# A delta-rule scan whose GpSimd arithmetic goes to VectorE, with joint loads and stored zeros, and one clearing tied behind the first gather of an expert stage

## The chip, the cores and the metric

The kernel runs on one core of a Trainium2 chip. The metric is the device time of one execution in microseconds (us), as the median of several. Engine names: PE is TensorE (matrix products; PEld its weight loads), DVE is VectorE, ACT is ScalarE, POOL is GpSimd, SP is SyncE, which here only issues DMAs. Each engine works through its own instructions in a fixed order; an instruction that waits holds up all behind it on its engine.

## The reference

One layer of a streaming encoder over 2048 tokens of width 1024, all in float32:

```
h = rms_norm(x) * (1 + scale1) + shift1
proj = h @ w_in                      # q,k,v of attention | q,k,v,z,beta,a of the delta rule | branch gates
o_a = diff_attention(q, k, v, lam)   # 4 heads, two 64-wide maps each, ALiBi bias, block-causal mask
o_b = gated_delta_rule(...)          # 4 heads, state 128 x 128 per head, chunks of 64 tokens
merged = gate_a * (o_a @ w_branch_a) + gate_b * (o_b @ w_branch_b)
x = x + gate1 * (merged @ w_out)
x = x + gate2 * hier_moe(rms_norm(x) * (1 + scale2) + shift2)   # top 2 of 32 SwiGLU experts
```

The delta rule of one chunk, per head:

```
lower = strict_lower(beta_i * (k @ k^T) * decay);  a_mat = I + lower
u, w  = solve(a_mat, [v * beta, k * beta * exp(gcum)])
v_new = u - w @ state
o     = (q * exp(gcum)) @ state + (lower_incl(q @ k^T) * decay) @ v_new
state = state * exp(gcum_last) + (k * exp(gcum_last - gcum))^T @ v_new
```

The expert layer sorts the tokens by expert, gathers their rows, runs `(silu(x @ w1[e]) * (x @ w3[e])) @ w2[e]` and adds the weighted results to the output rows.

## The kernel before

Large products run as three products of rounded parts (`hh`, `hl` of the activations, `ghi`, `glo` of the weights). The stages follow each other: projections (to about 780 us of the trace), `gates_and_gdn` (780 to 1300), attention with the merge of the branches (to 1900), output projection and router (to 2105), the routing tables, and from about 2150 the experts (`phase5`).

`gates_and_gdn` interleaves two kinds of work. A gate unit is a group of 24 PE matmuls `pg` of 512 columns (lines 554 to 556) with little work on other engines; they fill PE. The delta rule works on 16 blocks `t` of 128 tokens (two chunks each):

- `gdn_a(t)` (line 640) loads `kq` (keys and queries), makes the decay `e` on ACT, `el = e * sl` and `eu = e * triu` (masked copies) on POOL (lines 653, 654), then multiplies the products `pk` from PE into `el` and `eu` on DVE (lines 663, 665), and stores them to DRAM as `nL` and `qkm` from the SP queue.
- `lanes(hf)` (line 670), after the eighth and the sixteenth block, reads 32 x 32 diagonal blocks of `nL` of eight blocks `t` and inverts them by a recurrence on DVE: 31 pairs of a product `lQ` (line 682) and a sum (line 684), each needing the one before. The inverses `X` and their transposes `L` are stored to DRAM as `TB` and `UB`.
- `scan(t)` (line 694) loads these as `T` and `U` (tags sT, sU; eight DMAs of 16 KB, and eight clearings of 32 x 128 on POOL for the blocks beside the diagonal), `nw`, `kv` (keys, values), `zq`, and `kq` again; scales keys and values on POOL (lines 715, 716); completes the inverse by small PE products to 64 x 64, copied on POOL into `W` (lines 739, 740); then on the path from block to block: `pks` (keys times state), `R` on DVE (line 758), `pv` on PE (line 762), `vn` on ACT (line 764), `pS` on PE (line 767), the new state `S` on DVE (line 770). The output is normalised on DVE and ACT, transposed on PE and stored as `oTB` from the SP queue.

`nw`, `kv`, `zq` and the three tiles of `lanes` share five buffers (tag c4). `el`, `vn` and `oT` share the one buffer of tag el, `eu` and `o` that of tag eu (`GB = 1`). The order of instructions on each engine is set by a scheduler ahead of the run, not by the text.

In `phase5`, the row numbers of the first expert block (`sgi`) come out of the routing tables, a gather DMA from the POOL queue (line 1584) fetches its rows into `xfirst`, POOL clears a small tile `g` (line 1587), and a DVE copy of it, `gone` (line 1589), is set behind the routing's last instruction. The DVE work of the first expert (`ow`, and the first rounding remainders `low`, line 1620) is ordered behind `gone`. PE transposes `xfirst` (line 1694), ACT and DVE split it (`xh`, lines 1698 and 1699), and the expert's matmuls follow.

Of the kernel before, what the change touches and what calls it, by code (L numbers as in the profile page):

```python
# [9 lines left out]
F32 = mybir.dt.float32  # L10
# [4 lines left out]
ALU = mybir.AluOpType  # L15
# [66 lines left out]
class K:  # L82
# [65 lines left out]
    def phase1(self, late):  # L148
        tc, nc, I = self.tc, self.nc, self.i
        h3 = late.enter_context(tc.tile_pool(name="h3", bufs=1, reuse_waits="tile"))  # L150
        d = self.d = {}
        for n in ("q_hi", "q_lo", "k_hi", "k_lo"):
            d[n] = self.dram(n, (H, P, S))
        d["v_tok"] = self.dram("v_tok", (S, 512))
        d["gqT"] = self.dram("gqT", (H, P, S))
        d["gkT"] = self.dram("gkT", (H, P, S))
        d["gk_tok"] = self.dram("gk_tok", (S, 512))
        d["gv_tok"] = self.dram("gv_tok", (S, 512))
        d["zs"] = self.dram("zs", (S, 512))
        d["mods"] = self.dram("mods", (4, D))  # L160
        d["gate"] = self.dram("gate", (2, KT, P, S))
        with ExitStack() as ctx:
# [105 lines left out]
            for j in range(2):  # L268
# [8 lines left out]
                if j == 0:  # L277
                    first = make_h(0, xs.pop(0))
# [157 lines left out]
            def gdn_unit(which, w, h, s, ct):  # L436
# [37 lines left out]
                if which != "q":  # L474
                    nc.scalar.dma_start(
                        d[f"g{which}_tok"][s * TS:(s + 1) * TS, h * P:(h + 1) * P]
                        .rearrange("(a p) b -> p a b", p=P),
                        tok.rearrange("p (a b) -> p a b", b=P))
                if which != "v":
                    yield 1  # L480
                    yield 1
                    t2 = ps.tile([P, 512], F32, tag="tp", bufs=3, name=f"c2{which}{h}{s}")
                    for t in range(4):
                        nc.tensor.transpose(t2[:, t * P:(t + 1) * P], tok[:, t * P:(t + 1) * P], self.ident)
                    o = wk.tile([P, 512], F32, tag="e3", name=f"co{which}{h}{s}")
                    nc.scalar.copy(o, t2)
                    nc.scalar.dma_start(d[f"g{which}T"][h, :, s * TS:(s + 1) * TS], o)

# [73 lines left out]
    def gates_and_gdn(self, ctx, sm, ps, hxp, hh, hl):  # L562
# [5 lines left out]
        qk = self.dram("qkm", (NT, P, H, P))  # L568
        TB = self.dram("TB", (NT, H, 4, 32, 32))
        UB = self.dram("UB", (NT, H, 4, 32, 32))  # L570
        c = E(tc.tile_pool(name="cg", bufs=1, reuse_waits="tile"))
# [9 lines left out]
        def sm64(name):  # L581
            return c.tile([P, NT, H], F32, name=name)
# [9 lines left out]
        bt = lambda a: a.unsqueeze(1).to_broadcast([P, NT, H])  # L592
        beta, g, x, e1, e2, e3 = (sm64(n) for n in ("beta", "g", "gx", "ge1", "ge2", "ge3"))
        A.activation(beta, self.ba[:, :, 0:4], AF.Tanh, scale=0.5)
# [7 lines left out]
        V.tensor_scalar(out=e2, in0=e2, scalar1=-1.0, scalar2=None, op0=ALU.add)  # L602
        z0 = sm64("gz0")
        V.tensor_scalar(out=z0, in0=e2, scalar1=0.0, scalar2=None, op0=ALU.is_equal)
# [26 lines left out]
        G.memset(S0, 0.0)  # L631
        state = [S0]

        def load_kq(t):
            kq = hxp.tile([P, H, 2, P], F32, tag="hx", name=f"kq{t}")
            for j, n in enumerate(("gkT", "gqT")):
                nc.sync.dma_start(kq[:, :, j, :], d[n][:, :, t * P:(t + 1) * P].rearrange("h p t -> p h t"))
            return kq

        def gdn_a(t):  # L640
# [8 lines left out]
            A.activation(e, e, AF.Exp, scale=-1.0)  # L649
            el = gd.tile([P, H, P], F32, tag="el", name=f"el{t}", bufs=GB)  # L650
            eu = gd.tile([P, H, P], F32, tag="eu", name=f"eu{t}", bufs=GB)
            mb = lambda a: a.unsqueeze(1).to_broadcast([P, H, P])
            G.tensor_tensor(out=el, in0=e, in1=mb(self.sl), op=ALU.mult)
            G.tensor_tensor(out=eu, in0=e, in1=mb(self.triu), op=ALU.mult)
            yield 1
            for hp in range(2):
                pk = psg(f"pk{t}_{hp}").rearrange("p (h j t) -> p h j t", h=2, j=2)
                for hh in range(2):
                    h = 2 * hp + hh
                    PE.matmul(pk[:, hh], kq[:, h, 0, :], kq[:, h], start=True, stop=True)  # L660
                for hh in range(2):
                    h = 2 * hp + hh
                    V.scalar_tensor_tensor(out=el[:, h, :], in0=pk[:, hh, 0, :], scalar=nbeta[:, t, h:h + 1],
                                           in1=el[:, h, :], op0=ALU.mult, op1=ALU.mult)
                V.tensor_tensor(out=eu[:, 2 * hp:2 * hp + 2, :], in0=pk[:, :, 1, :],
                                in1=eu[:, 2 * hp:2 * hp + 2, :], op=ALU.mult)
            nc.sync.dma_start(nL[t].rearrange("h i j -> i h j"), el)
            nc.sync.dma_start(qk[t], eu)

        def lanes(hf):  # L670
            X = gd.tile([P, 32, 32], F32, tag="c4", name=f"lX{hf}", bufs=5)
            L = gd.tile([P, 32, 32], F32, tag="c4", name=f"lL{hf}", bufs=5)
            Q = gd.tile([P, 1024], F32, tag="c4", name=f"lQ{hf}", bufs=5)
            src = nL[8 * hf:8 * hf + 8].rearrange("t h r c -> (t h) r c")
# [14 lines left out]
            for dst, src in ((TB, X), (UB, L)):  # L689
                dv = dst[8 * hf:8 * hf + 8].rearrange("t h b r c -> (t h) b r c")  # L690
                for b in range(4):
                    nc.sync.dma_start(dv[:, b], src[32 * b:32 * b + 32])

        def scan(t):
            c4 = lambda n: gd.tile([P, 2, H, P], F32, tag="c4", name=f"{n}{t}", bufs=5)
            nw, kv, zq = c4("nw"), c4("kv"), c4("zq")
# [11 lines left out]
            nc.sync.dma_start(qm, qk[t])  # L708
# [52 lines left out]
            for h in range(H):  # L761
                PE.matmul(pv[:, h * P:(h + 1) * P], W[:, h, :], R[:, h, :], start=True, stop=True)
            vn = gd.tile([P, H, P], F32, tag="el", name=f"vn{t}", bufs=GB)
            A.copy(f2(vn), pv)
# [9 lines left out]
            for h in range(H):  # L774
                PE.matmul(pq[:, h * P:(h + 1) * P], kq[:, h, 1, :], S0[:, h, :], start=True, stop=True)
            o = gd.tile([P, H, P], F32, tag="eu", name=f"o{t}", bufs=GB)
            for h in range(H):
# [17 lines left out]
            for h in range(H):  # L795
                PE.transpose(tp[:, h * P:(h + 1) * P], o[:, h, :], self.ident)
            oT = gd.tile([P, H, P], F32, tag="el", name=f"oT{t}", bufs=GB)
# [767 lines left out]
    def phase5(self):  # L1565
# [3 lines left out]
        with ExitStack() as ctx:  # L1569
# [13 lines left out]
            first = wk.tile([P, D], F32, tag="x", name="xfirst")  # L1583
            G.indirect_dma_start(out=first[0:P // 2], out_offset=None, in_=d["h2"],
                                 in_offset=bass.IndirectOffsetOnAxis(ap=self.gi[0:P // 2, b0:b0 + 1], axis=0))

            G.memset(g0, 0.0)
            with tc.issue_after(self.routed.ins):
# [261 lines left out]
```

## Time and profile before

| what | value |
|---|---|
| median of 3 executions | 2963.07 us (2959.84 to 2963.28) |
| profiled execution, its own time | 2976.06 us |
| its span in the trace | 2974.1 us |
| mean granted TensorE clock | 0.976 of full speed |
| PE / DVE / ACT / POOL busy | 94% / 72% / 45% / 12% |
| mean DMA rate | 189 GB/s |

The profile is of one execution. The span runs from the first to the last instruction. [...] Idle time of an engine costs only where another one waits for its next instruction.

### The profile page before, as it was taken

The numbers are of one execution on the slowest core, as the hardware profiler recorded it, in microseconds if no ns is written. First come the engines' busy times: TensorE is split into PE (matmuls) and PEld (weight loads), VectorE is DVE, ScalarE is ACT, GpSimd is POOL, SyncE is SP. The second block draws the span as 40 slices with busy tenths as digits, with TensorE's granted clock in tenths as the row PEclk, the third lists the DMA queues.
The fourth block names the chain that finished last, engine by engine and source line by source line (L and its number), as shares of the span: only waits on it lengthen the run. The fifth ranks groups of instructions, "written<-read, shape, count | busy, mean of one in ns | idle before, by whom it ended". The sixth has DMA issues, their size and how long they took to land. (4 is left out here: it accounts for less than half of the span.)

```text
span 2974.1 us, 43868 instructions
## 1 busy us (share of the span) xinstructions
PE 2793.6 (94%) x14845; PEld 2268.2 (76%) x14845; DVE 2130.4 (72%) x5098; ACT 1326.5 (45%) x2409; POOL 356.7 (12%) x354
## 2 busy tenths in 40 slices
PE   5999999999999899999999999999689999999997
PEld 4888778788787777777787887788567777777776
DVE  7567668996355643457888786687787797897896
ACT  4522213332322243356765564322255465664664
POOL 2300000000122122200000000100032121122211
PEclk8999999999999999999999999999789999999999
DMA  6333572211455465487776756744488898998995
GB/s 227 111 99 114 164 228 72 93 61 54 117 164 147 139 184 164 137 175 173 182 180 168 186 145 174 223 158 153 150 296 273 265 338 274 328 333 266 310 356 165
DMA packets 426243, 561.18 MB, mean 189 GB/s; under 512 B 56520, under 2 KB 240920, under 8 KB 426016
## 3 DMA queue, kind: packets, MB, share of 16 engines
q1 hardware_dynamic: 340560, 440.87, 48.3%
q10 hardware_dynamic: 73744, 75.53, 7.4%
q0 software_dynamic: 11712, 41.95, 6.1%
q8 instruction: 119, 1.95, 0.3%
q14 instruction: 108, 0.88, 0.1%
HBM read 436.06 MB, written 122.18 MB: 188 GB/s over the span
## 5 line engine op out<-in xcount | busy, mean ns | idle before, releaser
L1620 DVE TENSOR_TENSOR low<-raww,hiw 128x1024 fp32r<-128x1024 f32 x384 | 445.8, 1218 | 20.1 <-ACT hiw L1618 19.1
L1618 ACT CAST hiw<-raww 128x1024 fp32r<-128x1024 f32 x384 | 379.2, 1049 | 133.7 <-PE py L1673 68.3
L554 PE MATMUL pg<-hh,ghi 128*128 128x512 f32 x512 | 209.7, 410 | 2.5 <-ACT ghi L545 2.5
L338 PE MATMUL mma<-whi,hh 128*128 128x512 f32 x512 | 209.5, 409 | 2.7 <-ACT hh L245 1.4
L1010 DVE CUSTOM_DVE_ANT_0 sp<-sc,M 128x512 f32<-128x512 f32 (+1 forms) x320 | 183.7, 606 | 38.2 <-PE sc L1008 37.5
L556 PE MATMUL pg<-hh,glo 128*128 128x512 f32 x512 | 207.3, 405 | 0.0
L555 PE MATMUL pg<-hl,ghi 128*128 128x512 f32 x512 | 207.1, 404 | 0.0
L340 PE MATMUL mma<-whi,hl 128*128 128x512 f32 x512 | 203.6, 398 | 1.1 <-DVE hl L255 0.8
L339 PE MATMUL mma<-wlo,hh 128*128 128x512 f32 x512 | 202.4, 395 | 0.4 <-DVE wlo L261 0.4
L1015 ACT ACTIVATE sp<-sp,mx 128x128 f32<-128x128 f32 (+15 forms) x128 | 153.9, 1203 | 51.8 <-DVE mx L1013 45.9
L1034 PEld LDWEIGHTS av<-V,aT 128*128 128x128 f32 x1088 | 138.2, 192 | 33.8 <-ACT aT L1032 26.3
L348 PE MATMUL mmb<-hh,whi 128*128 128x512 f32 x384 | 156.4, 407 | 5.3 <-ACT whi L260 5.3
L1034 PE MATMUL av<-V,aT 128*128 128x128 f32 x1088 | 152.3, 282 | 9.2 <-ACT aT L1032 8.1
L350 PE MATMUL mmb<-hh,wlo 128*128 128x512 f32 x384 | 151.7, 395 | 0.5 <-POOL wlo L261 0.4
L349 PE MATMUL mmb<-hl,whi 128*128 128x512 f32 x384 | 151.0, 393 | 0.0
L1007 PE MATMUL sc<-K,qd 128*128 128x512 f32 (+1 forms) x320 | 130.7, 412 | 6.9 <-DVE mx L1010 2.9
L1032 ACT COPY aT<-tr 128x512 f32<-128x512 f32 (+3 forms) x160 | 78.4, 517 | 99.0 <-PE tr L1030 98.6
L1008 PE MATMUL sc<-K,ql 128*128 128x512 f32 (+1 forms) x320 | 117.7, 375 | 1.7 <-DMA ql<-q_lo 1.7
L1672 PE MATMUL py<-hiw,dh 128*128 128x512 f32 x272 | 108.8, 400 | 10.5 <-ACT dh L1663 10.3
L338 PEld LDWEIGHTS mma<-whi,hh 128*128 128x128 f32 x512 | 97.7, 191 | 25.1 <-ACT hh L245 1.8
L340 PEld LDWEIGHTS mma<-whi,hl 128*128 128x128 f32 x512 | 97.5, 190 | 24.3 <-DVE hl L255 1.7
L1628 POOL DMA_INDIRECT x<-h,sgi x34 | 72.0, 2118 | 356.6 <-PE tx L1635 210.0
(550 smaller groups left out, 7127.5 us busy)
## 6 DMA issues: line engine op xcount, KB each, us to landing
raww<-in_w_dram SPq DMA_DIRECT2D x384, 512.0 KB, 7.5
mw<-in_w_ada_dram SPq DMA_DIRECT2D x64, 256.0 KB, 4.2
gate<-gt ACTq DMA_DIRECT2D x64, 256.0 KB, 2.9
g<-gate SPq DMA_DIRECT2D x64, 256.0 KB, 5.4
graw<-in_w_in_dram SPq DMA_DIRECT2D x52, 256.0 KB, 4.7
raw<-in_w_in_dram SPq DMA_DIRECT2D x22, 512.0 KB, 4.5
K<-k_hi SPq DMA_DIRECT2D x36, 256.0 KB, 5.1
K<-k_lo SPq DMA_DIRECT2D x36, 256.0 KB, 7.4
```

The lines of the kernel that those rows point to most:

```text
L338: nc.tensor.matmul(pt[:, :n], a, his[k][:, :n], start=(k == 0), stop=False)
L339: nc.tensor.matmul(pt[:, :n], a, los[k][:, :n], start=False, stop=False)
L340: nc.tensor.matmul(pt[:, :n], b, his[k][:, :n], start=False, stop=(k == KT - 1))
L348: nc.tensor.matmul(pt, a, hh[s][:, k, :], start=(k == 0), stop=False)
L554: nc.tensor.matmul(pt, hi[:, k, :], hh[:, k, :], start=(k == 0), stop=False)
L555: nc.tensor.matmul(pt, hi[:, k, :], hl[:, k, :], start=False, stop=False)
L556: nc.tensor.matmul(pt, lo[:, k, :], hh[:, k, :], start=False, stop=(k == KT - 1))
L1010: V.tensor_tensor_reduce(out=b[:, k0:k0 + n], in0=pt[:, :n], in1=Mt[:, mo:mo + n], op0=ALU.add, op1=ALU.min, scale=SLOPES[h], scalar=3e38, ...
L1015: A.activation(b[:, :nk], b[:, :nk], AF.Exp, bias=mm, scale=-1.0, accum_out=(l1, l2)[m][:, j:j + 1])
L1034: PE.matmul(av[:, :P], aT[:, k * P:(k + 1) * P], Vt[k4 // 4][:, k, :], start=(k4 + k == 0), stop=(k4 + k == qt))
L1618: A.copy(hi, raw)
L1620: V.tensor_tensor(out=lo, in0=raw, in1=hi.bitcast(F32), op=ALU.subtract)
```

## The change

In the delta rule:

- The masked copy `el` is gone: the DVE operation of line 663 reads `e` itself, so that `el` is no longer zero above the diagonal. `eu = e * triu` moves to DVE, as do the two scalings of `kv` and the two copies into `W`. POOL keeps one clearing of 64 x 256 a scan.
- `T` and `U` come in one DMA each, zeros included: `TB` and `UB` hold 128 x 64 per block and head, and 16 DMAs of 256 KB on the POOL queue write zeros into them once, ahead of `gdn_a`. The stores of `X` and `L` put 32 x 32 blocks between the zeros.
- `kq` and `kv` come in one DMA of 512 KB each instead of two of 256 KB.
- The stores of `nL` and `qkm` go to the POOL queue, that of `oTB` to the ACT queue.
- Tags el and eu get two buffers.

In `phase5` the clearing of `g` is tied behind the gather of `xfirst` on POOL; it stood ahead of it in the schedule.

```
-            G.tensor_tensor(out=el, in0=e, in1=mb(self.sl), op=ALU.mult)
-            G.tensor_tensor(out=eu, in0=e, in1=mb(self.triu), op=ALU.mult)
+            el = gd.tile([P, H, P], F32, tag="el", name=f"el{t}", bufs=2)
+            eu = gd.tile([P, H, P], F32, tag="eu", name=f"eu{t}", bufs=2)
+            V.tensor_tensor(out=eu, in0=e, in1=self.triu.unsqueeze(1).to_broadcast([P, H, P]), op=ALU.mult)
...
-            nc.sync.dma_start(nL[t].rearrange("h i j -> i h j"), el)
-            nc.sync.dma_start(qk[t], eu)
+            nc.gpsimd.dma_start(nL[t].rearrange("h i j -> i h j"), el)
+            nc.gpsimd.dma_start(qk[t], eu)
...
+        for dst in (TB, UB):
+            for n in range(8):
+                nc.gpsimd.dma_start(dst[2 * n:2 * n + 2].rearrange("t h (p q) c -> (t h p) (q c)", q=8),
+                                    S0.rearrange("p h c -> p (h c)"))
...
-            for b in range(4):
-                pb, o = slice(32 * b, 32 * b + 32), 32 * (b % 2)
-                nc.sync.dma_start(T[pb, :, o:o + 32], TB[t, :, b].rearrange("h r c -> r h c"))
-                nc.sync.dma_start(U[pb, :, o:o + 32], UB[t, :, b].rearrange("h r c -> r h c"))
-                G.memset((U if b % 2 else T)[pb, :, 32 - o:64 - o], 0.0)
+            for a, src in ((U, UB), (T, TB)):
+                nc.sync.dma_start(a, src[t].rearrange("h p c -> p h c"))
...
-            nc.sync.dma_start(f2(kt), d["gk_tok"][r, :])
-            nc.sync.dma_start(f2(vt), d["gv_tok"][r, :])
+            nc.sync.dma_start(kv.rearrange("p j h c -> p (j h c)"), d["gkv"][r].rearrange("p j c -> p (j c)"))
...
-            G.tensor_tensor(out=vt, in0=vt, in1=hb(beta), op=ALU.mult)
-            G.tensor_tensor(out=kt, in0=kt, in1=hb(kds), op=ALU.mult)
+            V.tensor_tensor(out=vt, in0=vt, in1=hb(beta), op=ALU.mult)
+            V.tensor_tensor(out=kt, in0=kt, in1=hb(kds), op=ALU.mult)
...
-            G.tensor_copy(W[0:64, :, 0:64], U[0:64])
-            G.tensor_copy(W[64:128, :, 64:128], U[64:128])
+            V.tensor_copy(W[0:64, :, 0:64], U[0:64])
+            V.tensor_copy(W[64:128, :, 64:128], U[64:128])
...
-            nc.sync.dma_start(d["oTB"][:, :, r].rearrange("h p t -> p h t"), oT)
+            nc.scalar.dma_start(d["oTB"][:, :, r].rearrange("h p t -> p h t"), oT)
...
-            G.memset(g0, 0.0)
+            with tc.issue_after(rows.ins):
+                G.memset(g0, 0.0)
             with tc.issue_after(self.routed.ins):
                 gone = V.tensor_copy(self.gone, g0)
```

POOL at the start of the expert stage, before; `xfirst` and `x` are gathers, `zr` is an earlier tile:

```order
L1185 MEMSET zr 128x1024
L1587 MEMSET g_21249 1x1
L1584 DMA xfirst<-h_18359,sgi 64x1024
L1628 DMA x_21333<-h_18359,sgi 128x1024
L1628 DMA x_21374<-h_18359,sgi 128x1024
```

And now:

```order
L1182 MEMSET zr 128x1024
L1581 DMA xfirst<-h_18143,sgi 64x1024
L1585 MEMSET g_21033 1x1
L1626 DMA x_21117<-h_18143,sgi 128x1024
L1626 DMA x_21158<-h_18143,sgi 128x1024
```

The clearing of `g`, which `gone` copies on DVE, now stands behind the gather. The order on DVE around `gone` is the same in both.

DVE at the end of the second `lanes`, before; `R` and `S` are those of the first scan:

```order
L682 TENSOR_TENSOR lQ_8356<-lX_8354,lL_8355 128x900
L546 TENSOR_TENSOR glo_9449<-graw_9454,ghi_9448 128x512
L684 TENSOR_REDUCE lX_8354<-lQ_8356 128x30
L682 TENSOR_TENSOR lQ_8356<-lX_8354,lL_8355 128x961
L684 TENSOR_REDUCE lX_8354<-lQ_8356 128x31
L758 SCALAR_TENSOR_TENSOR R_8600<-pks_8595,nbeg,kv_8400 128x128 x4
L770 SCALAR_TENSOR_TENSOR S_8617<-S_7199,egl,pS_8612 128x128 x4
```

And DVE now, in the same recurrence; `R_8552` is the first scan's, `R_8770` and `kv_8530` the second's, and the whole of the first scan's DVE work lies between the two pieces:

```order
L685 TENSOR_REDUCE lX_8330<-lQ_8332 128x15
L755 SCALAR_TENSOR_TENSOR R_8552<-pks_8547,nbeg,kv_8376 128x128
L683 TENSOR_TENSOR lQ_8332<-lX_8330,lL_8331 128x256
...
L685 TENSOR_REDUCE lX_8330<-lQ_8332 128x27
L712 TENSOR_TENSOR kv_8530<-kv_8530,beta 128x512
L713 TENSOR_TENSOR kv_8530<-kv_8530,kds 128x512
L683 TENSOR_TENSOR lQ_8332<-lX_8330,lL_8331 128x784
L755 SCALAR_TENSOR_TENSOR R_8770<-pks_8765,nbeg,kv_8530 128x128
L685 TENSOR_REDUCE lX_8330<-lQ_8332 128x28
L755 SCALAR_TENSOR_TENSOR R_8770<-pks_8765,nbeg,kv_8530 128x128 x3
```

Before, the first scan's `R` came behind the whole recurrence; now three scans run within it (the third's `R` comes 17 rows after its end). On PE, the first scan's `pv` stood 277 rows behind the last block's `pk`; now it stands 125 rows behind it, and between that `pk` and the third scan's `pv` lie 220 gate matmuls. The following scans have about 20 gate matmuls each between them instead of 25.

## Rows read from the trace of the kernel before

**Rows 1.** The page, part 1: busy time, share of the span, instructions of each engine

```profile
PE 2793.6 (94%) x14845; PEld 2268.2 (76%) x14845; DVE 2130.4 (72%) x5098; ACT 1326.5 (45%) x2409; POOL 356.7 (12%) x354
```

**Rows 2.** Windows: from:to and length, busy time per engine, granted clock, DMA share, GB/s

```profile
780.00:1300.00 520.00, 495.12 (x3322) 400.50 (x3321) 243.29 (x689) 170.10 (x423) 111.99 (x196) 0.99 0.54 155
880.00:920.00 40.00, 34.66 (x156) 28.78 (x155) 34.18 (x46) 10.60 (x22) 11.41 (x10) 0.91 0.45 138
947.10:997.70 50.60, 48.40 (x262) 37.88 (x260) 42.95 (x68) 9.70 (x22) 1.57 (x6) 1.00 0.39 112
970.00:990.00 20.00, 20.00 (x88) 16.07 (x87) 19.48 (x20) 3.13 (x6) 0.00 (x0) 1.00 0.22 67
1000.00:1050.00 50.00, 45.10 (x403) 35.96 (x404) 24.09 (x84) 18.61 (x51) 14.18 (x30) 0.94 0.57 172
1050.00:1300.00 250.00, 239.86 (x1905) 191.47 (x1904) 101.95 (x369) 91.56 (x238) 49.28 (x119) 1.00 0.56 158
2200.00:2974.10 774.10, 742.69 (x3465) 584.50 (x3463) 631.41 (x719) 457.50 (x579) 164.63 (x87) 0.99 0.89 291
```

**Rows 3.** Waits of PE from 780 to 1290: us in total, times, longest

```profile
PE pv L762 <- DVE R L758: 9.0, 4, 7.4
PE pg L644 <- DVE eu L665: 5.3, 2, 3.5
PE pS L767 <- ACT vn L764: 4.4, 4, 1.7
PE pS L767 <- issue: 1.7, 1, 1.7
```

**Rows 4.** Timeline, end of the second lanes: start, length, operation, count [idle before, releaser]

```profile
996.44 1.15 DVE L684 TENSOR_REDUCE lX<-lQ 128x31 f32<-128x961 f32 x1
...
1000.36 1.04 POOL L716 TENSOR_TENSOR kv<-kv,kds 128x512 f32<-128x512 f32 x1 [37.60 <-DMA kv<-gk_tok]
...
1002.43 0.87 DVE L758 SCALAR_TENSOR_TENSOR R<-pks,nbeg,kv 128x128 f32<-128x128 f32 x3 [4.84 <-POOL kv L715]
...
1002.93 0.55 PE L762 MATMUL pv<-R,nw 128*128 128x128 f32 x1 [7.43 <-DVE R L758]
```

**Rows 5.** Timeline, start of the experts

```profile
2151.73 0.13 DVE L1589 COPY gone<-g 1x1 f32<-1x1 f32 x1
...
2152.58 9.67 POOL L1584 DMA_INDIRECT xfirst<-h,sgi  x1 [42.94 <-DVE gone L1589]
...
2156.63 4.61 DVE L1620 TENSOR_TENSOR low<-raww,hiw 128x1024 fp32r<-128x1024 f32 x4
...
2162.55 0.98 POOL L1628 DMA_INDIRECT x<-h,sgi  x1 [0.30 <-issue]
...
2169.69 1.11 PE L1694 MATMUL tx<-ident,xfirst 64*128 64x64 f32 x8 [18.61 <-DMA xfirst<-h,sgi]
...
2170.82 0.42 DVE L1699 TENSOR_TENSOR xh<-tx,xh 128x256 fp32r<-128x256 f32 x1 [9.58 <-ACT xh L1698]
```

**Rows 6.** Groups on DVE, 780 to 1290: one

```profile
L546 DVE TENSOR_TENSOR glo<-graw,ghi 128x512 fp32r<-128x512 f32 x34 | 24.6, 727 | 54.3 <-ACT ghi L545 54.3
```

**Rows 7.** Groups on POOL, 780 to 1290: count, busy, mean ns, idle before

```profile
L654 POOL TENSOR_TENSOR eu<-e,triu 128x512 f32<-128x512 f32 x16 | 22.6, 1416 | 0.6 <-DVE glo L546 0.6
...
L716 POOL TENSOR_TENSOR kv<-kv,kds 128x512 f32<-128x512 f32 x16 | 16.8, 1051 | 99.5 <-DMA kv<-gk_tok 68.2 <-ACT vn L764 14.8 <-PE po L781 8.8
...
L740 POOL COPY nw<-sU 64x256 f32<-64x256 f32 x16 | 6.6, 415 | 12.4 <-ACT sU L735 7.8 <-issue 2.4 <-POOL nw L739 1.6
```

**Rows 8.** Timeline, DVE: the same product in the first and the second lanes

```profile
896.05 2.24 DVE L682 TENSOR_TENSOR lQ<-lX,lL 128x729 f32<-128x729 f32 x1
...
982.65 1.52 DVE L682 TENSOR_TENSOR lQ<-lX,lL 128x729 f32<-128x729 f32 x1
```

**Rows 9.** Windows, matmuls of line 554 alone (a third of a gate unit's)

```profile
1050.00:1300.00 250.00, 78.08 (x189) 35.85 (x190) 1.00 0.56 158
```

**Rows 10.** DMA issues from 780 to 1290: engine, count, KB each, median us to landing

```profile
nL<-el SPq DMA_DIRECT2D x16, 256.0 KB, 2.9
```

More of the change, by code (lines that the diff above doesn't have):

```diff
@@ L58 @@
 C_Z, C_BA, C_G = 3072, 3584, 3592
+NC4 = 5
 def pipeline(units, old_first=False):
@@ L154, in phase1 @@
         d["v_tok"] = self.dram("v_tok", (S, 512))
[L155 to L158, printed above, removed]
+        d["gkq"] = self.dram("gkq", (H, 2, P, S))
+        d["gkv"] = self.dram("gkv", (S, 2, 512))
         d["zs"] = self.dram("zs", (S, 512))
@@ L475, in gdn_unit @@
                     nc.scalar.dma_start(
-                        d[f"g{which}_tok"][s * TS:(s + 1) * TS, h * P:(h + 1) * P]
+                        d["gkv"][s * TS:(s + 1) * TS, "kv".index(which), h * P:(h + 1) * P]
                         .rearrange("(a p) b -> p a b", p=P),
@@ L486, in gdn_unit @@
                     nc.scalar.copy(o, t2)
-                    nc.scalar.dma_start(d[f"g{which}T"][h, :, s * TS:(s + 1) * TS], o)
+                    nc.scalar.dma_start(d["gkq"][h, "kq".index(which), :, s * TS:(s + 1) * TS], o)
             def mod_unit(j, hf):
@@ L592, in gates_and_gdn @@
         bt = lambda a: a.unsqueeze(1).to_broadcast([P, NT, H])
-        beta, g, x, e1, e2, e3 = (sm64(n) for n in ("beta", "g", "gx", "ge1", "ge2", "ge3"))
+        beta, g = (sm64(n) for n in ("beta", "g"))
+        tmp = wk.tile([P, 8, NT, H], F32, tag="gt", name="gtmp")
+        x, e1, e2, e3, z0 = (tmp[:, n] for n in range(5))
         A.activation(beta, self.ba[:, :, 0:4], AF.Tanh, scale=0.5)
@@ L632, in gates_and_gdn @@
         state = [S0]
+        for dst in (TB, UB):
+            for n in range(8):
+                nc.gpsimd.dma_start(dst[2 * n:2 * n + 2].rearrange("t h (p q) c -> (t h p) (q c)", q=8),
+                                    S0.rearrange("p h c -> p (h c)"))
         def load_kq(t):
             kq = hxp.tile([P, H, 2, P], F32, tag="hx", name=f"kq{t}")
-            for j, n in enumerate(("gkT", "gqT")):
-                nc.sync.dma_start(kq[:, :, j, :], d[n][:, :, t * P:(t + 1) * P].rearrange("h p t -> p h t"))
+            nc.sync.dma_start(kq.rearrange("p h j t -> p (h j) t"),
+                              d["gkq"][:, :, :, t * P:(t + 1) * P].rearrange("h j p t -> p (h j) t"))
             return kq
@@ L663, in gdn_a @@
                     V.scalar_tensor_tensor(out=el[:, h, :], in0=pk[:, hh, 0, :], scalar=nbeta[:, t, h:h + 1],
[L664 removed]
+                                           in1=e[:, h, :], op0=ALU.mult, op1=ALU.mult)
                 V.tensor_tensor(out=eu[:, 2 * hp:2 * hp + 2, :], in0=pk[:, :, 1, :],
                                 in1=eu[:, 2 * hp:2 * hp + 2, :], op=ALU.mult)
[L667 to L668 removed]
+            nc.gpsimd.dma_start(nL[t].rearrange("h i j -> i h j"), el)
+            nc.gpsimd.dma_start(qk[t], eu)
         def lanes(hf):
[L671 to L673 removed]
+            X = gd.tile([P, 32, 32], F32, tag="c4", name=f"lX{hf}", bufs=NC4)
+            L = gd.tile([P, 32, 32], F32, tag="c4", name=f"lL{hf}", bufs=NC4)
+            Q = gd.tile([P, 1024], F32, tag="c4", name=f"lQ{hf}", bufs=NC4)
             src = nL[8 * hf:8 * hf + 8].rearrange("t h r c -> (t h) r c")
@@ L689, in lanes @@
             for dst, src in ((TB, X), (UB, L)):
-                dv = dst[8 * hf:8 * hf + 8].rearrange("t h b r c -> (t h) b r c")
+                dv = dst[8 * hf:8 * hf + 8].rearrange("t h p c -> (t h) p c")
                 for b in range(4):
-                    nc.sync.dma_start(dv[:, b], src[32 * b:32 * b + 32])
+                    o = 32 * (b % 2)
+                    nc.sync.dma_start(dv[:, 32 * b:32 * b + 32, o:o + 32], src[32 * b:32 * b + 32])
         def scan(t):
-            c4 = lambda n: gd.tile([P, 2, H, P], F32, tag="c4", name=f"{n}{t}", bufs=5)
+            c4 = lambda n: gd.tile([P, 2, H, P], F32, tag="c4", name=f"{n}{t}", bufs=NC4)
             nw, kv, zq = c4("nw"), c4("kv"), c4("zq")
@@ L762, in scan @@
                 PE.matmul(pv[:, h * P:(h + 1) * P], W[:, h, :], R[:, h, :], start=True, stop=True)
-            vn = gd.tile([P, H, P], F32, tag="el", name=f"vn{t}", bufs=GB)
+            vn = gd.tile([P, H, P], F32, tag="el", name=f"vn{t}", bufs=2)
             A.copy(f2(vn), pv)
@@ L775, in scan @@
                 PE.matmul(pq[:, h * P:(h + 1) * P], kq[:, h, 1, :], S0[:, h, :], start=True, stop=True)
-            o = gd.tile([P, H, P], F32, tag="eu", name=f"o{t}", bufs=GB)
+            o = gd.tile([P, H, P], F32, tag="eu", name=f"o{t}", bufs=2)
             for h in range(H):
@@ L796, in scan @@
                 PE.transpose(tp[:, h * P:(h + 1) * P], o[:, h, :], self.ident)
-            oT = gd.tile([P, H, P], F32, tag="el", name=f"oT{t}", bufs=GB)
+            oT = gd.tile([P, H, P], F32, tag="el", name=f"oT{t}", bufs=2)
             A.activation(f2(oT), tp, AF.Copy, scale=gnb)
-            nc.sync.dma_start(d["oTB"][:, :, r].rearrange("h p t -> p h t"), oT)
+            nc.scalar.dma_start(d["oTB"][:, :, r].rearrange("h p t -> p h t"), oT)
         def units():
@@ L1583, in phase5 @@
             first = wk.tile([P, D], F32, tag="x", name="xfirst")
-            G.indirect_dma_start(out=first[0:P // 2], out_offset=None, in_=d["h2"],
-                                 in_offset=bass.IndirectOffsetOnAxis(ap=self.gi[0:P // 2, b0:b0 + 1], axis=0))
-            G.memset(g0, 0.0)
+            rows = G.indirect_dma_start(out=first[0:P // 2], out_offset=None, in_=d["h2"],
+                                        in_offset=bass.IndirectOffsetOnAxis(ap=self.gi[0:P // 2, b0:b0 + 1], axis=0))
+            with tc.issue_after(rows.ins):
+                G.memset(g0, 0.0)
             with tc.issue_after(self.routed.ins):
```

13 lines of the change are left out of this document (3 added, 10 removed).

## The prediction

> **What bounds the kernel.** The page's first part says PE: busy for 94% of the span, with DVE at 72%, ACT 45% and POOL 12% [rows 1]. That is an average over stages, so I read the windows next, one stretch for each place that the change touches. In the stage of the gates and the delta rule (780 to 1300) PE is busy 495.12 of 520.00 us [rows 2]: idle time of 24.9 us is all that an edit there can recover directly. The granted clock adds a little. It is 0.91 over the 40 us from 880 and 0.94 over the 50 us from 1000, and 1.00 elsewhere [rows 2]; both dips follow a PE stall. At full clock these stretches would lose some 0.09 x 40 + 0.06 x 50 = 6.6 us less, so the stage holds about 31 us for everything. The waits of PE say who ends its idle time: `R` on DVE ahead of `pv`, 9.0 us, 7.4 of them in one stall; `eu` on DVE ahead of `pg`, 5.3; `vn` on ACT ahead of `pS`, 4.4, and another 1.7 there without a releaser [rows 3]. The timeline shows the large stall: the second `lanes` ends on DVE at 996.44 + 1.15, the load of the first scan's `kv` takes the buffer that this frees, POOL scales it from 1000.36, `R` starts at 1002.43 and PE at 1002.93 after 7.43 idle [rows 4].
>
> The second place is the start of the experts. PE waits 18.61 us for the gathered rows `xfirst` [rows 5], and from 2200 on it is busy 742.69 of 774.10 us [rows 2], so a start that comes earlier is kept to the end unless DMA (0.89 busy there) gives part of it back.
>
> **Start of the experts.** The gather starts at 2152.58 and holds POOL for 9.67 us. It ends at 2162.25, about 1 us after DVE falls idle at 2156.63 + 4.61 = 2161.24; the next gather starts at 2162.55, with DVE idle, and takes 0.98 [rows 5]. So I read 8.69 of the 9.67 us as time lost to DVE running beside it. From the gather's end to the transposes of `xfirst` it is 2169.69 − 2162.25 = 7.44 us. Now the clearing stands behind the gather, `gone` behind the clearing, and all the DVE work of the first expert behind `gone`: DVE has only three or four tiny operations left while the gather is issued. Then the gather ends at 2152.58 + 0.98 = 2153.56, its rows land at 2153.56 + 7.44 = 2161.0. DVE pays for it: the block that lay between `gone` (2151.86) and 2161.24, 9.4 us, starts at about 2153.8 and ends at 2163.2. `xh` on DVE stands behind that block, so PE's matmuls begin after 2163.2 instead of 2170.82: 7.6 us earlier. Of the 9.6 us DVE was idle [rows 5], 2 are spent up front. The bounds: if the gather is long for another reason, DVE starts behind it, 11 us late, and the block then ends near 2171.7, 1 us later than `xh` now: a loss of about 1. Above, all of the 8.69 would be a gain. I take 7.5, nearest to the row with DVE idle. What is late next: the second gather now meets a busy DVE. If it takes 9.67 from 2153.8 and 7.44 to land, its rows are there at 2171, and in the trace now they are not needed in the 10 us behind `xh`; that is tight but covered.
>
> [...]
>
> **POOL's arithmetic on DVE.** Added are 16 masks `eu` and 32 scalings, 128x512 with two inputs in SBUF; the nearest row is `glo`, 727 ns [rows 6]: 48 x 0.73 = 35 us. Added are 32 copies of 64x256, which took 415 ns on POOL [rows 7]; I take 0.4 each, 12.8 us (at least 0, at most the 0.73 of the larger tile: 23). DVE goes from 243.29 to about 291 of 520 us, 56%. POOL loses its arithmetic: `eu` 22.6, one scaling 16.8, one copy 6.6 us and their like [rows 7], off the path except where DVE or PE waited for it. There is a return: the product `lQ` of 128x729 took 2.24 us in the first `lanes`, where POOL computes, and 1.52 in the second, where it does not [rows 8].
>
> First `lanes` (880 to 920): DVE is busy 34.18 of 40 us and PE idle 5.34 [rows 2]. Each `gdn_a` there adds 0.73 and gives back about as much in products that no longer stretch. I take 0, between +2 and −2.
>
> Second `lanes`: before, its 50.6 us hold 42.95 us of DVE and 48.40 of PE [rows 2], and PE then stalls 7.43. Now three scans run inside. A scan's price on DVE: 1050 to 1300 has 13 scans (104 matmuls `pS`) and 16 `glo`; (101.95 − 16 x 0.73) / 13 = 7.0 us [rows 2, 6], plus 1.46 and 0.8 for what comes from POOL: 9.2. A scan's price on PE: a stretch of gate matmuls alone has 88 in 20 us, 0.227 each [rows 2]; three times 189 of them lie in the 250 us [rows 9], so (239.86 − 567 x 0.227) / 13 = 8.5 us. From the last `pk` to the third `pv` PE has 220 x 0.227 + 2.7 x 8.5 = 73 us. DVE starts `lanes` some 11 us after that `pk` (its own products 1.5, the store 2.9 [rows 10], four loads about as long each but overlapping, and their issue), then needs 42.95 + 2.3 x 7.0 + 3 x 2.2 = 66, in all 77. So PE waits for DVE some 4 us, or 5 with the places where the interleave is uneven, against 9.0 before in all waits for `R` [rows 3]; with a little of the 3 us of clock from 1000 to 1050 I take a gain of 4.5. Bounds: DVE with the dear copies and one more scan's worth of waiting loses 4; no wait at all gains 9.0 and 3 of clock, 12.
>
> **Second buffers and joint loads.** `vn` no longer waits for the store of `oT` from a shared buffer: 4.4 and 1.7 us in front of `pS` [rows 3] are open; part becomes the plain latency of ACT's copy, because now only 4 gate matmuls (0.9 us) stand between `pv` and `pS`. I take 2 gained, between 5 and −3. The third to sixth scans have 20 gate matmuls, 20 x 0.227 + 8.5 = 13.0 us of PE against 9.2 plus one `glo` on DVE: covered. Eight loads and eight clearings less a scan free SP and POOL, neither on the path after the first scan.
>
> **Zeros and stores from POOL.** 16 stores of 256 KB, 4 MB, ahead of the stage, and 32 stores from a queue that the trace shows for gathers only. An issue costs between 0.98 (undisturbed) and 9.67 us (DVE beside it) [rows 5], on a POOL that has nothing else to do. I take the lower end and nothing on PE's path: PE has gate units, and POOL is 12% busy [rows 1].
>
> **The sum.** 7.5 + 0 + 4.5 + 2 = 14; I take 1 off for DMA late in the experts: 13 of the profiled execution's 2976.06 us, 0.44%. It lies 13 us above the median of 2963.07, so the same share gives 2950.1; I predict 2950.5.
>
> **Rivals.** *DVE eats the stage* (0.17): the first and second `lanes` lose 2 and 4, the scans 1, and only the experts' start stays: 7.5 − 7, about 2962.5. For it: DVE busy 19.48 of 20 us at 970 to 990 [rows 2], before any scan is added. Against it: PE is idle there now at 1000, with nothing to lose twice. *The gather is not freed* (0.13): its time is its queue's own and not DVE's; −1 + 6.5 gives 2957.5. Against it speaks the 0.98 next to the 9.67. *Stores from POOL come late and the change is slower* (0.12): the last two stores of `nL` are issued beside a busy DVE, each up to 8.7 us late, 17.4 together. The second `lanes` stands ahead of the first scan's `R` in DVE's order, so PE waits 17.4 us more at the first `pv`, minus the 4.5 and with 3 us of clock: 7.5 + 2 − 20.4 + 1 = 10 slower, 2973. It decides once a store is more than about 5 us late. The trace has one disturbed issue, of 9.67 [rows 5]. [...] *All idle time goes* (0.16): 7.5 + 12 + 5 + 2, 26.5: 2936.5.
>
> **Chances.** The forecast has 0.42, with a range of its own of 2943 to 2957. This kernel's measurement can tell 0.2%, 5.9 us, from no change: faster means below 2957.1, slower above 2969. Faster: nearly all of the forecast (0.41), the last rival (0.16), half of the second (0.06) and some of the first (0.03): 0.66. Slower: most of the third and a tail of the first: 0.12. The same: 0.22. The range of 2936 to 2966 leaves out the third rival and half of the fourth.
>
> **What would show it.** The gather of `xfirst` at about 1 us on POOL, `gone` behind it, `xh` some 9.5 us after `gone` and PE's wait for `xfirst` near 10 instead of 18.61. No wait of 7 us at the first `pv`, but several of 1 to 3 us for `R` between the last `pk` and the fourth scan; few waits of `pS` for `vn`. DVE near 291 us in the stage, POOL under 15. The `lQ` of 128x729 at 1.5 us in both `lanes`. Wrong, if POOL's stores take several microseconds each and `lL` loads come late, if the first wait for `R` exceeds 8 us, or if the gather stays near 9 us with DVE idle.

## The result and the profile after

The changed kernel takes 2946.78 us (2943.25 to 2949.28), against 2963.18 for the kernel before on the same chip: a ratio of 0.9931, 95% interval 0.9915 to 0.9947. The quotient of these two medians, of four executions each, is 0.9945. A second measurement beside other kernels gave 0.9929 (0.9912 to 0.9946), with medians of 2947.82 and 2967.86. It is faster, by 0.7%; the profiled execution has a span of 2947.6 us, its own time 2949.28, against 2974.1 and 2976.06.

| landmark in the trace, us | before | after |
|---|---|---|
| first `pg` to last `pg` of the decay | 137.5 | 136.2 |
| first `pg` to first `sc` of attention (the stage) | 519.0 | 504.4 |
| start of the gather to first expert matmul | 18.7 | 11.0 |
| first to last expert matmul of that line | 740.2 | 742.2 |

The windows of the stage, before and then after: from:to and length, busy time of PE, PEld, DVE, ACT, POOL, clock, DMA share, GB/s. Each begins at its own first `pg` and ends at its own first `sc`.

```profile
778.80:916.30 137.50, 132.16 (x633) 111.29 (x632) 69.42 (x154) 42.75 (x101) 40.51 (x34) 0.98 0.53 157
916.30:1050.00 133.70, 124.30 (x799) 98.89 (x798) 71.92 (x166) 36.52 (x85) 22.21 (x43) 0.97 0.51 147
1050.00:1297.80 247.80, 237.66 (x1893) 189.53 (x1891) 100.28 (x359) 90.13 (x231) 49.28 (x119) 1.00 0.56 157
```

```profile
776.10:912.30 136.20, 131.62 (x633) 110.29 (x632) 75.08 (x168) 42.21 (x101) 19.26 (x30) 0.99 0.51 156
912.30:1050.00 137.70, 129.88 (x887) 102.73 (x886) 81.31 (x209) 39.59 (x98) 5.56 (x12) 0.98 0.61 166
1050.00:1280.50 230.50, 229.62 (x1803) 185.16 (x1801) 111.48 (x383) 86.91 (x220) 6.54 (x30) 1.00 0.56 166
```

Idle time of PE is length less busy time: 5.3, 9.4 and 10.1 us before, 4.6, 7.8 and 0.9 after. Most of the 11.6 us came from behind 1050, where the scans follow each other; PE's busy time fell by 3.0 more, from 494.1 to 491.1 us, at granted clocks of 0.98, 0.97 and 1.00 before and 0.99, 0.98 and 1.00 after. In the kernel before, a gate matmul took 0.63 us from 906.8 to 909.8, at a granted clock of 0.50 (905 to 910), and 0.39 us from 970 to 990, at 1.00. Single executions differ: the first experiment, whose stage has the code of before, idles 5.4, 9.5 and 7.5 us in these windows, and two more executions of the changed stage idle 6.1, 7.6 and 1.2 (second experiment) and 4.5, 7.0 and 3.1 (the last). From one to the other kernel the stage thus loses 7.5 to 11.6 us of idle time, 4.4 to 9.2 of them behind 1050. The waits of PE in the stage that answer to [rows 3]:

```profile
PE pk L661 <- ACT e L650: 2.5, 1, 2.5
PE p L745 <- ACT A L742: 1.8, 1, 1.8
PE pa L721 <- DMA nw<-nL: 1.6, 2, 1.1
PE pv L759 <- DVE R L755: 1.5, 1, 1.5
PE pg L646 <- ACT e L650: 1.2, 1, 1.2
```

No wait of `pS` for `vn` is left, and one for `R`. At the experts' start, which answers to [rows 5]:

```profile
2130.35 0.97 POOL L1581 DMA_INDIRECT xfirst<-h,sgi  x1 [236.25 <-DMA raww<-in_w_dram]
2131.34 0.09 POOL L1585 MEMSET g<- 1x1 f32 x1
2131.47 0.14 DVE L1587 COPY gone<-g 1x1 f32<-1x1 f32 x1 [1.62 <-POOL g L1585]
...
2133.05 1.04 POOL L1626 DMA_INDIRECT x<-h,sgi  x1 [1.61 <-DVE g L1589]
2133.14 0.53 DVE L1514 TENSOR_TENSOR ow<-eq,wl 128x368 fp32r<-128x368 f32 x1
...
2134.26 1.11 PE L1692 MATMUL tx<-ident,xfirst 64*128 64x64 f32 x8 [5.35 <-DMA xfirst<-h,sgi]
...
2135.64 6.11 POOL L1626 DMA_INDIRECT x<-h,sgi  x1 [1.56 <-PE tx L1692]
...
2136.30 4.62 DVE L1618 TENSOR_TENSOR low<-raww,hiw 128x1024 fp32r<-128x1024 f32 x4
...
2141.32 0.79 PE L1705 MATMUL pa<-hiw,xh 128*128 128x512 f32 x1 [5.94 <-DVE xh L1697]
```

The gather takes 0.97 us where it took 9.67, and DVE's 1.62 idle is the price. The rows reach the transposes 3.9 us after the gather's start; DVE's block, now behind `gone`, is what the first matmul waits for: PE sits idle for 5.94 us until `xh`. The next two gathers now stand beside that block. The second starts among the `ow` and takes 1.04 us all the same; the third takes 6.11 and ends 0.83 us behind the last of the four `low`. No wait of PE for either is in the trace.

### The profile page after: what moved, and what is told of

Read it like the earlier page. It is cut to its first block, busy times and chain, and to the rows that moved or that the text cites. A ratio compares the mean times of both kernels' runs of the same rounds, so it can differ in the third digit from the quotient of the medians.

```text
span 2947.6 us, 43496 instructions
## 1 busy us (share of the span) xinstructions
PE 2788.8 (95%) x14845; PEld 2266.8 (77%) x14845; DVE 2156.8 (73%) x5178; ACT 1326.0 (45%) x2409; POOL 283.9 (10%) x241
## 5 line engine op out<-in xcount | busy, mean ns | idle before, releaser
L1644 PE MATMUL pa<-low,xh 128*128 128x512 f32 x272 | 108.9, 400 | 5.7 <-DVE low L1618 5.7
```

## Experiments

Ratios are to the kernel before, on the same chip, with 95% intervals. "Stage" is the stretch of the table, in one profiled execution; the kernel before has 519.0 there and 516.3 in the first experiment, whose stage is the same code; the changed one 504.4, 505.7 (second experiment) and 505.8 (last).

**The tie alone, and all but the tie.**

```
# e1_tie_only, on the kernel before; e2_no_tie undoes it in the changed one
+            rows = G.indirect_dma_start(out=first[0:P // 2], out_offset=None, in_=d["h2"],
...
-            G.memset(g0, 0.0)
+            with tc.issue_after(rows.ins):
+                G.memset(g0, 0.0)
```

> The kernel before with one edit: the clearing of g is tied behind the gather of xfirst. First theory (DVE's products stretch the gather): the gather takes 1.0 us on POOL instead of 9.67, the first expert matmul comes 12 to 13 us after the end of the routing tables (2150.7 to 2171.3 before, so 20.6), that is 7.5 us earlier, and the whole kernel gains 5 to 7.5 us: 2956 to 2958. Second theory (the gain at the experts' start is given back behind it, where DMA is busy 0.89): the first matmul is as early, but the stretch from it to the end grows by more than 4 us and the kernel gains under 3.5.

> The changed kernel without the tie, the clearing ahead of the gather again; all else as changed. First theory: the gather takes 9 to 10 us, the first expert matmul comes 20 to 21 us after the tables, and the kernel is 5 to 7.5 us slower than the changed one: 2952 to 2954. Second theory (given back): under 3.5 us slower.

Measured: 0.9972 (0.9961 to 0.9984) for the tie alone, 0.9963 (0.9948 to 0.9978) for all but the tie. The two add up to the whole. The gather takes 1.12 us with the tie, 9.57 without; from its start to the first matmul it is 11.1 and 18.1 us. From the first to the last expert matmul of that line it is 740.5 us with the tie alone, where before has 740.2, and 742.6 without it, where the changed kernel has 742.2: nothing is given back. The second theory falls; the tie is worth about 8 us.

**Second buffers, taken out and put in alone.**

```
# e3_one_buf, on the changed kernel (also for eu, vn, o, oT); e4_two_buf the reverse on the kernel before
-            el = gd.tile([P, H, P], F32, tag="el", name=f"el{t}", bufs=2)
+            el = gd.tile([P, H, P], F32, tag="el", name=f"el{t}", bufs=GB)
```

> The changed kernel with one buffer each for the tags el and eu; all else as changed, the scans still start inside the second lanes. First theory (the second buffers removed the wait of vn for the store of oT, which spaced pv and pS): ACT waits over 15 us for that store again, PE's idle time behind 1050 us rises from 0.9 to 7 to 10 us, the kernel is 5 to 9 us slower: 2952 to 2956. Second theory (the later scans gain because they start earlier and are spread over more gate matmuls): PE idles under 3 us there and the kernel is within 3 us of the changed one.

> The kernel before with second buffers for the tags el and eu (and the small gate tiles of the start packed into one tile, to make room); POOL keeps its arithmetic, stores and loads are as before, the first scan still comes behind the second lanes. First theory (buffers): PE's idle time behind 1050 us falls from 10.1 to under 3, the 7.4 us stall at the first pv stays, the kernel gains 6 to 9 us: 2954 to 2957. Second theory (early start of the scans): idle time behind 1050 stays at 7 to 10, the kernel gains under 2.

Measured: 0.9989 (0.9975 to 1.0004) without the buffers, 0.9996 (0.9984 to 1.0007) with them alone. Without them the changed kernel loses nearly all it had won, although the tie in it still works (its gather takes 0.98 us): the tie alone had 0.9972, so the rest of the change without the buffers likely costs some 5 us. Its stage is 524.7 us, longer than before. ACT's idle time ahead of `vn`, without second buffers and then in the changed kernel:

```profile
  PE pv L759: 24.8, 8
  DMA oTB<-oT: 20.9, 8
```

```profile
  PE pv L759: 36.5, 16
```

So the wait of `vn` for the store of `oT` is real, 20.9 us in 8 of 16 scans, and the first theory holds for it. PE's idle time behind 1050 is 7.0 us there. But the loss is larger than expected (some 17 us). The stage is 20.3 us longer than the changed one: 6.1 us of idle time behind 1050, 3.3 more in the first `lanes`, 2.3 between, and 8.7 of PE's busy time, with a granted clock of 0.78 from 937 to 960 and 0.90 from 1200 to 1250.

The buffers alone do half of what I expected: idle time behind 1050 is 3.9 us (7.5 and 10.1 with the old stage), but PE idles 8.8 us from 943 to 998, where the first `pv` waits 6.8 for `R`, and the stage of 514.5 us is only 2 to 4 shorter. No gain in time can be told. First theory right in direction, wrong in size.

**Joint loads and stored zeros alone.**

```
# e7_loads_zeros: the changed kernel with POOL's arithmetic, the mask sl, one buffer, SP stores and no tie
+            G.tensor_tensor(out=el, in0=e, in1=mb(self.sl), op=ALU.mult)
+            G.tensor_tensor(out=eu, in0=e, in1=mb(self.triu), op=ALU.mult)
...
+            nc.sync.dma_start(nL[t].rearrange("h i j -> i h j"), el)
```

> The kernel before with the joint loads of kq, kv, T and U and the stored zeros alone: arithmetic and masks on POOL, one buffer each for the tags el and eu, all stores of blocks from SP, no tie. Three scans run within the second lanes as in the changed kernel, though later (the first pv stands 229 gate matmuls behind the last pk; 305 before, 120 changed). First theory (without second buffers the early scans gain little, their waits only move): the 7.4 us stall is gone, waits of pS for vn of 5 us or more stay, the stage is 512 to 520 us (516 to 519 before), the kernel within 4 us of before. Second theory (the early start of the scans is the gain): the stage is under 510 us, the kernel gains over 6.

Measured: 0.9993 (0.9983 to 1.0003), stage 520.3 us. The large stall goes: PE idles 5.5 us from the last `pg` to 1050, where before has 9.4. It comes back as smaller ones, 14.3 us behind 1050 against 7.5 to 10.1:

```profile
PE pS L769 <- ACT vn L766: 9.0, 7, 2.8
PE pg L649 <- DVE eu L671: 5.4, 2, 3.6
PE otp L798 <- DVE o L793: 3.2, 3, 1.3
```

The loads and zeros bring three scans into the second `lanes`; the buffers remove waits of the kind that the loads and zeros alone run into. Each alone is worth nothing that can be told; together with the stores and without the copy `el`, POOL's other arithmetic left in place (next, 0.9942 less the tie), they make some 9 us. No run has the buffers and the joint loads and nothing else.

**Arithmetic back on POOL; stores back on SP.**

```
# e5_pool_arith, also for kt and the two copies into W
-            V.tensor_tensor(out=eu, in0=e, in1=self.triu.unsqueeze(1).to_broadcast([P, H, P]), op=ALU.mult)
+            G.tensor_tensor(out=eu, in0=e, in1=self.triu.unsqueeze(1).to_broadcast([P, H, P]), op=ALU.mult)
...
-            V.tensor_tensor(out=vt, in0=vt, in1=hb(beta), op=ALU.mult)
+            G.tensor_tensor(out=vt, in0=vt, in1=hb(beta), op=ALU.mult)
# e6_stores_sp
-            nc.gpsimd.dma_start(nL[t].rearrange("h i j -> i h j"), el)
-            nc.gpsimd.dma_start(qk[t], eu)
+            nc.sync.dma_start(nL[t].rearrange("h i j -> i h j"), el)
+            nc.sync.dma_start(qk[t], eu)
```

> The changed kernel with the arithmetic back on POOL: the mask of eu, the two scalings of kv, the two copies into W; loads, stored zeros, stores, buffers and tie as changed. First theory (DVE was free enough, and POOL's arithmetic costs DVE and PE through longer products and later operands): the product of 128x729 in the first lanes takes about 2 us again, DVE falls by 30 to 35 us of busy time in the stage, the stage from its first pg to the first sc grows from 504.4 by 2 to 6 us. Second theory (the move to DVE cost what DVE took on in the second lanes): the stage is 2 to 5 us shorter, for PE idles less from 940 to 1000.

> The changed kernel with the stores of nL and qkm from the SP queue again; all else as changed. First theory (stores from POOL are neutral, 0.76 and 0.54 us of a POOL that has nothing else): the stage is within 2 us of 504.4 and the kernel within 3 us. Second theory (SP's queue was in the way of loads, and the move gave part of the gain): the stage grows by 3 to 6 us, with new waits for DMA ahead of pk or pa.

Measured: 0.9942 (0.9929 to 0.9955) with the arithmetic on POOL, stage 510.5, DVE busy 238.65 us there against 267.87. The stage is 5 to 6 us longer, as the first theory has it, but the intervals of the whole overlap: by the ratios the move of the arithmetic is worth 3 to 4 us, which time alone does not show. One sign of the first theory misses: the product of 128x729 in the first `lanes` stays at 1.51 us. Other products are stretched there, the one before it most. In this run, and then in the changed kernel:

```profile
887.53 2.89 DVE L683 TENSOR_TENSOR lQ<-lX,lL 128x676 f32<-128x676 f32 x1
...
891.35 1.51 DVE L683 TENSOR_TENSOR lQ<-lX,lL 128x729 f32<-128x729 f32 x1
```

```profile
890.12 1.43 DVE L683 TENSOR_TENSOR lQ<-lX,lL 128x676 f32<-128x676 f32 x1
...
892.74 1.52 DVE L683 TENSOR_TENSOR lQ<-lX,lL 128x729 f32<-128x729 f32 x1
```

The 31 products of the first `lanes` together take 27.3 us with POOL's arithmetic, 23.7 without, and 25.5 in the kernel before; the sum tells it and the one row doesn't.

Stores on SP: 0.9949 (0.9935 to 0.9963), stage 518.1 us, 12 longer, in a profiled execution that was the slowest of six (2962.66 us, median 2956.63). Its trace shows the place. SP's queue there, and below it the same loads in the changed kernel:

```profile
909.62 3.53 SPq L694 DMA_DIRECT2D TB<-lX  x4
913.38 3.53 SPq L694 DMA_DIRECT2D UB<-lL  x4
...
929.81 0.82 SPq L668 DMA_DIRECT2D nL<-el  x1
...
936.00 6.21 SPq L677 DMA_DIRECT2D lL<-nL  x4
```

```profile
908.39 3.22 SPq L694 DMA_DIRECT2D TB<-lX  x4
912.08 8.70 SPq L694 DMA_DIRECT2D UB<-lL  x4
925.29 2.38 SPq L677 DMA_DIRECT2D lL<-nL  x4
```

Queued on SP behind the stores of the inverses, the last `nL` leaves at 929.81 instead of 920.80, and the second `lanes` gets its loads 10.7 us later (9.8 after taking off that the last `pk` is 0.9 later too). PE then waits 5.67 us in one place for a gate weight that SP loaded behind them; the waits ahead of `pk` and `pa` that the second theory named are not there. That is its mechanism in another place, and larger than it said in this execution; over the runs, 0.9949 against 0.9931 and 0.9929 is a likely loss of 5 us whose interval still touches none.

**A second buffer for `e`.**

```
# e8_e_two: e, R, osq with bufs=2; eu, o with bufs=1
# e9_e_in_tu:
-            e = gd.tile([P, H, P], F32, tag="e", name=f"e{t}", bufs=GB)
+            e = gd.tile([P, H, P], F32, tag="sT", name=f"e{t}", bufs=2)
...
+            TU = gd.tile([P, 2, H, 64], F32, tag="sT", name=f"sT{t}", bufs=2)
+            T, U = TU[:, 0], TU[:, 1]
```

> The changed kernel with two buffers for e (and R, osq) and one for eu (and o); el keeps two. In the changed kernel ACT may not write the next e before DVE has read the last one, and PE waits 3.7 us for e in the first lanes. First theory: these waits go, the stage is 2 to 4 us shorter than 504.4, and the later scans stay without waits, so that it is the second buffer of el that they need: the kernel is 2 to 5 us faster than the changed one. Second theory (eu's second buffer carries the later scans' gain, by o): PE idles 4 us or more behind 1050 and the kernel is slower than the changed one.

> The changed kernel with a second buffer for e in place of the wait that the change made: e takes the two buffers that T and U use later, T and U sharing one tile of each. First theory (in the first lanes ACT waits to write e until DVE has read the last one): the waits of PE for e, 3.7 us, fall under 1, the stretch from the first to the last pg is 2 to 3 us shorter than 136.2, the kernel 2 to 4 us faster than the changed one. Second theory (DVE bounds the first lanes, and the wait for e only shows it): waits for eu or el take its place, the stretch is within 1 us.

Measured: 0.9945 (0.9932 to 0.9958) and 0.9929 (0.9909 to 0.9948). The first is not 2 to 5 us faster than the changed kernel but likely some 4 slower (the intervals overlap), and its stage is 516.6 us, 11 to 12 longer, in the slowest of its five executions (2961.12 us, median 2954.95): PE idles 18.9 us in it against 13.3 to 14.9, and is busy 6.6 longer, with a granted clock of 0.93 from 911 to 1050, where the changed kernel has 0.98. Waits for `e` are gone, but `pg` waits 5.1 us for the single `eu`, as in the kernel before [rows 3]; idle time behind 1050 is 2.0 us, so the later scans do without the second buffer of eu, while the first `lanes` need it. In the second, the stretch to the last `pg` is 133.7 us, 2.4 shorter than in the last run of the changed kernel (136.1), the first theory's number. But PE idles only 0.3 us less there (4.2 against 4.5), for `pg` waits 4.2 us for `eu` on DVE, as the second theory has it; the other 2.1 are PE's busy time, at a granted clock of 1.00 against 0.99. The stage is 507.0 us against 505.8:

```profile
PE pg L646 <- DVE eu L666: 4.2, 2, 2.3
PE pa L721 <- DMA nw<-nL: 2.6, 3, 1.3
PE p L745 <- ACT A L742: 2.1, 1, 2.1
```

Most of what is won early is lost at the first scan: counted from the first `pg`, its `kv` load leaves 1.6 us earlier than in the changed kernel, and its `pv` starts 0.5 earlier. Neither version beats the changed kernel.

**What stretches a gather.**

```
# e10_sums, on the changed kernel without the tie
+                    if i == 0 and n != "w2" and k < 4:
+                        r6 = 6 if n == "w1" and k == 0 else 1
+                        V.tensor_reduce(out=sink[:, 0:r6], in_=raw.unsqueeze(1).to_broadcast([P, r6, 1024]), axis=AX.X,
+                                        op=ALU.add)
```

> The changed kernel without the tie, so that the gather of xfirst runs beside DVE again; of the first expert's remainders the first four are left out (the rounded weights stand in for them) and DVE does sums of one input instead, the first one over 128x6144 elements. DVE's products with two inputs in SBUF (g, ow) then end about 4.9 us after gone, and the sum lasts some 6.5 us more. First theory (DVE instructions that read two inputs from SBUF stretch the gather): the gather ends about 1 us behind the last ow, 5 us after its start. Second theory (any DVE work does): it ends about 1 us behind the sum, 11 to 12 us after its start.

This run leaves four remainders out and was executed once, so only the gather is read. POOL's gathers, and the DVE operations beside them:

```profile
2127.42 5.03 POOL L1581 DMA_INDIRECT xfirst<-h,sgi  x1 [42.04 <-DMA raww<-in_w_dram]
2132.75 0.99 POOL L1632 DMA_INDIRECT x<-h,sgi  x1 [0.30 <-issue]
```

```profile
2131.07 0.52 DVE L1514 TENSOR_TENSOR ow<-eq,wl 128x368 fp32r<-128x368 f32 x1
2131.52 6.53 DVE L1621 TENSOR_REDUCE sink<-raww 128x6 f32<-128x6144 f32 x1
```

The gather ends at 2132.45, 0.86 us behind the last product, while the sum of 6.53 us goes on until 2138.05; the next gather takes 0.99 us beside that sum. The first theory holds for this gather, the second falls. The second gather of the changed kernel, 1.04 us among the `ow`, shows that not every gather beside such products is held; it is 1.03 to 1.05 us in all eight traces with the tie. What lets it through is not shown.

**The changed kernel again.**

> The changed kernel itself once more, beside the others: 0.990 to 0.995 of the kernel before, the stage 503 to 507 us from the first pg to the first sc by both theories.

Measured: 0.9929 (0.9912 to 0.9946), stage 505.8 us, with 14.6 us of idle time of PE.

## Why the prediction was right

The direction, the size (13 us forecast, 16 by the medians, some 20 by the ratio) and one of its two places hold as forecast; the other, 6.5 forecast for the stage, came out about twice as large (10.5 to 14.6 us between the executions), by a term that I had set too low. That 16 lies so near to 13 is partly luck: 2963.18 is the lowest of the four medians that the kernel before has in these measurements (the others 2967.86 to 2969.79), and the 20 us of the second measurement are half as much again as forecast.

- *Experts' start*: 7.5 forecast. The gather took 0.97 us, and from its start to the first matmul 11.0 us instead of 18.7: 7.8 us. The tie alone makes 8 us of the whole, with an interval of 5 to 12. The rows land 2.9 us behind the issue's end and not 7.44; I had taken that from the disturbed gather, and why it is shorter is not shown. The sum does not feel it, because DVE's block ends later than the rows land. The price that I named, DVE's start behind the gather, is there (1.62 us). I took off 1 us for DMA; the tie's runs show no such loss (the stretch over the experts is 0.3 us longer with the tie alone, 0.4 shorter in the changed kernel; the table's 742.2 is one execution, and the last experiment has 739.5). The rival that the gather's time is its queue's own falls with the 0.97 us and with the sums.
- *First `lanes`*: 0 forecast. The stretch is 1.3 us shorter than before's, and 0.2 shorter than in the first experiment (136.4): right. The product of 128x729 takes 1.52 us there instead of 2.24, as forecast [rows 8], but that row was a poor witness, for it stays short with POOL's arithmetic too; the 31 products together came down by 1.8 us. The new wait of ACT for `e` was not forecast; it took 3.7 us of PE in the place of 5.3 for `eu`.
- *Second `lanes`*: 4.5 forecast, as DVE waits of 5 us against 9.0. Idle time from the last `pg` to 1050 fell by 1.6 us (1.9 and 2.5 in the other executions), and PE's busy time by 3.0 over the whole stage, which I put down to the clock: about the size forecast if all of that is counted here. But not as I told it: DVE's `R` ends only one wait of 1.5. DVE began the second `lanes` 12.5 us behind the last `pk` (11 taken) and was busy for 53.2 of its 63.7 us, where I had 66 of work. PE reached the third `pv` 83.2 us behind that `pk`, where I had 73. The rest is the chain of the first scan itself: its `kv` holds DVE up 5.17 us until the joint load lands, and PE waits for its loads and for ACT's copies between small products.

```profile
943.98 0.69 DVE L712 TENSOR_TENSOR kv<-kv,beta 128x512 f32<-128x512 f32 x1 [5.17 <-DMA kv<-gkv]
```

- *Second buffers*: 2 forecast, between 5 and −3, and here the step was mis-sized. Idle time behind 1050 fell from 10.1 (7.5 in the first experiment) to 0.9 us (1.2 and 3.1 in the other executions). I counted the two waits of `pS` in [rows 3], 6.1 us, and gave most of it back to the latency of ACT's copy (`vn`, 0.59 us each) behind 4 gate matmuls; that latency shows in no wait of PE. I priced the buffers and the early scans as separate small terms, and the buffers are worth much only beside the rest of the change: alone 0.9996, the early scans alone 0.9993, and taken out of the changed kernel the buffers cost some 17 us.
- *Costs on DVE*: its busy time rose from 241.6 to 267.87 us in the stage, not 291. The masks and scalings took 0.69 us each (0.73 taken), the copies 0.29 (0.4 taken), 42.3 in all. Of these 7.3 came back in shorter instructions, 2.3 of them in the products `lQ`, and 8.7 because more instructions overlap, which busy time counts once (their times add up to 24.0 us more than the busy time before, 32.7 now). POOL is busy 31.4 us and not under 15: its issues count, 20.9 us.
- *Stores from POOL*: nothing on the path, forecast and measured. The 32 issues took 0.76 and 0.54 us each, at the most 0.77 and 0.55; the `qkm` at 786.20, with DVE idle for 1.79 us up to 787.27, took 0.54 like the others:

```profile
L668 POOL DMA_DIRECT2D nL<-el x16 | 12.2, 761 | 144.2 <-DVE el L664 136.5 <-DVE lQ L683 7.7
L669 POOL DMA_DIRECT2D qkm<-eu x16 | 8.7, 542 | 0.7 <-DVE eu L666 0.7
```

The slower rival rested on the one disturbed issue of 9.67 us, and that price belongs to a gather. The plain stores show nothing of it: the store of `qkm` at 898.83 us lies wholly within a product `lQ` (898.43 to 900.06) and took 0.54 us. The first gather differs: 9.57 to 9.67 us beside products, 0.97 to 1.12 without; a gather beside a sum took 0.99. What in a gather waits is not shown, for no run here separates its parts, and the 1.04 us of the second gather stay unexplained.

What stays open: why the execution without the second buffers has the lower clock behind small stalls (0.78 from 937 to 960, where the changed kernel has 0.85), and how the gain of the stage splits between the loads, the stores and the arithmetic; those intervals overlap. The changed kernel also asks for `kv` ahead of `qkm` in each scan, which no run separates from the joint loads.

## What to carry to other kernels

A wait that is removed alone can be worth nothing, because the next one stands close behind it: price edits that act on one chain together, and test each both alone and taken out. Here the buffers alone had 0.9996 and the joint loads and zeros alone 0.9993. Where an engine waits for a gathered tile, look at what the vector engine does while the gather is issued: here it paid to hold products of two SBUF inputs back by 1.6 us, for the gather then took 0.97 us instead of 9.67. The later gathers of the same kernel, up to 8.6 us long beside such products, ended no wait of PE. A queue of loads and stores is a path too: one store behind eight others moved the loads that needed it by some 10 us.

## What the hardware showed that was not expected

- The issue of the first gather, where it ran beside DVE's products of two SBUF inputs, ended about 1 us behind the last of them: 9.67 us in the kernel before (1.0 behind), 5.03 where they ended early (0.86 behind); another gather took 0.99 us beside a sum. Not every gather was held: the second of the changed kernel took 1.04 us among such products, the third 6.11. A plain store from the same queue took 0.54 to 0.77 us beside products and sums.
- Stores of 32 x 32 blocks between the zeros, by their layout in pieces of 128 bytes instead of 4 KB, held SP longer, and unevenly: the eight of `L` 1.78 us each by the median (0.43 before), the eight of `X`, which go ahead of them, 0.56 (0.42 before). Here they lay off the path.
